# Stick-breaking attention summed by parts in a one-core encoder step

## The chip, the cores and the metric

The kernel runs on one core of a Trainium2 chip. The metric is the device time of one execution in microseconds (us); a kernel is run several times and the median is taken. A profiled execution gives the trace. The engines are named as in the profile: PE is the matrix engine, PEld its weight loads, DVE the vector engine, ACT the scalar engine, POOL the third elementwise engine, SP the engine that issues the DMAs.

## The reference, cut to what matters

One layer: a projection of 1056 rows (1024 prompt, 32 sample) by 1024 features, of which eight heads of 64 go to attention, then convolution, gates, an output projection, a feed-forward part and an embedding gate. The change touches the attention over the 1024 prompt rows:

```python
z = jnp.einsum('bqhd,bkhd->bhqk', q, k) * scale
mask = k_pos[None, :] < q_pos[:, None]
log_1m = jnp.where(mask, jax.nn.log_sigmoid(-z), 0.0)
tail = lax.cumsum(log_1m, axis=3, reverse=True) - log_1m
a = jnp.where(mask, jnp.exp(jax.nn.log_sigmoid(z) + tail), 0.0)
out = jnp.einsum('bhqk,bkhd->bqhd', a, v)
```

So the weight of key s is sigmoid(z_s) times the product of sigmoid(-z_j) over the later keys j that the query may see. All of it is float32. The keys and values of the prompt and the samples are outputs too.

## The kernel before

Nearly every matrix product is made of three: each float32 operand is split into a rounded part and a remainder ("hi" and "lo"), and hi·hi, hi·lo and lo·hi are summed in PSUM. The program has stages: the input projection (`seven`, by a scheme with seven half-size products for each pair of output blocks, some 264 columns a matmul), then attention, then the projections `oc` and `oa` of the two branches, `wo`, and the feed-forward part and the rest.

**Order.** Under `manual_schedule` the instructions of ACT, PE, DVE and POOL run in the order in which Python writes them. SP's order is chosen by the framework's scheduler. In the projection stage `run(body)` takes one step of the matrix work (for `seven`, 12 matmuls) and then one step of every generator in the list `side`, so a `yield` in `values` or `keys_or_queries` means: 12 matmuls later. The values are the sets i7 (blocks p = 0 and 1) and i10 (blocks 2 and 3). Their generator `values(p, m)` runs while the next set is multiplied; block 1 starts six steps after block 0.

**Values before.** `m` holds 128 value features (two heads) by 1056 rows. `values` scales it, waits three steps, transposes eight 128×128 blocks on PE through PSUM (`pt_v`) into `vt`, writes `vt` to the output, and for each of the two heads splits `vt` into a tile `vs` (hi in columns 0 to 63, lo in 64 to 127), which goes to the DRAM scratch `vd`. Attention reads it back as `vv`. The 32 sample rows are transposed too (`pts_v`).

**Buffers.** Tiles made by `blk` share a pool of 34 buffers of one size (`bpool`). A tile that takes over a buffer waits for everything that still reads it, a DMA out of it included. The transposes' PSUM tiles (`tps`) have two buffers.

**Attention before.** There are 64 steps (p, j, i): block p, head j, and 128 queries i against L = 128(i+1) keys. In step n, in the order "LSAFBFG", `scores` (S) makes z for step n and two sigmoids of it, r = sigmoid(-z) and s = sigmoid(z), and POOL sets the last 128 columns of both where a key is not earlier than the query; `weigh` (L) scans r of step n-1 from its last key backwards into running products and multiplies s by the products one to the right; `flip` (A and B) transposes s of step n-2 on PE and splits it into hi and lo parts `at`; for odd i, `gather` (G) multiplies the `at` of 256 queries by `vv`, lo and hi of each key block, into `av`, whose halves are added (through `avl`) into `oT`. For the lower 128 of the 256 queries the last key block is all masked: POOL sets that half to zero and the matmul still takes 256 columns. At F the generator `work` puts gate matmuls (`ps_g`, later `ps_pw`) between; how many go into which step is set by `pace`, with a load for each step made from four constants. The 32 sample queries (`samples`: `zs`, `ss`, `sr`, `avs`) are done beside the first steps.

Of the kernel before, what the change touches and what calls it, by code (L numbers as in the profile page):

```python
# [49 lines left out]
def tile_step(  # L50
# [1 line left out]
    tc: tile.TileContext,  # L52
    xf, xr_, pT, ckT, cache_v, vecs,
    w_in, w_attn_out, w_conv_out, w_o, w_up, w_down, w_ple_gate, w_ple,
    y_main, y_last, k_out, v_out, v_sample, conv_out,
):


# [8 lines left out]
    def blk(name, dt=F32, shape=None):  # L67
        return bpool.tile(shape or [P, T], dt, tag="B", name=name)
# [364 lines left out]
    ch, cl = [], []  # L433
    st, cst = {}, {}
    qsT, ksT, vsT = ([cpool.tile(sh, F32, name=f"{nm}s{p}") for p in range(4)] for nm, sh in (("q", [P, DEC]), ("k", [P, DEC]), ("v", [DEC, P])))

    def run_units(units):

# [63 lines left out]
    def values(p, m):  # L502
        scaled(m)
        for _ in range(3):
            yield
        tm = blk(f"vt{p}", F32, [P, 8, P])
        for q0 in (0, 4):
            pt = tps.tile([P, 4, P], F32, tag="tp", name=f"pt_v{p}_{q0}")
            for i in range(4):
                nc.tensor.transpose(pt[:, i, :], m[:, (q0 + i) * P : (q0 + i + 1) * P], ident)  # L510
            nc.scalar.copy(tm[:, q0 : q0 + 4, :], pt)
            yield
        pt = tps.tile([P, 4, P], F32, tag="tp", name=f"pts_v{p}")
        nc.tensor.transpose(pt[:DEC, 0, :], m[:, SEQ:], ident)
        nc.scalar.copy(vsT[p], pt[:DEC, 0, :])
        nc.sync.dma_start(v_out[p], tm)
        nc.sync.dma_start(v_sample[p], vsT[p])
        for j in range(2):
            vs = blk(f"vs{p}{j}", F32R, [P, 8, P])
            src = tm[:, :, 64 * j : 64 * j + 64]  # L520
            nc.scalar.copy(vs[:, :, 0:64], src)
            dve(vs[:, :, 64:128], src, vs[:, :, 0:64].bitcast(F32), op=sub)
            nc.sync.dma_start(vd[p, j], vs.bitcast(F32).rearrange("p a c -> p (a c)"))
            yield

    def conv_in(nb, m):

# [227 lines left out]
    def scores(p, j, i):  # L755
        q, kk = live["q", p, j, i // 2], st["k", p, j]
        L = P * (i + 1)
        nh = 1 if L <= 512 else 2
        W = L // nh
        z = zps.tile([P, 2, 512], F32, tag="z", name=f"z{p}{j}{i}")  # L760
        tq = slice((i % 2) * P, (i % 2) * P + P)
        for h in range(nh):
            zz = z[:, h, :W]
            ks = kk[:, h * W : (h + 1) * W]
            nc.tensor.matmul(zz, q[:, 0, tq], ks, start=True, stop=False)
            nc.tensor.matmul(zz, q[:, 1, tq], ks, start=False, stop=True)
        zv = z[:, :nh, :W]
        s = blk(f"s{p}{j}{i}", F32, [P, SEQ])
        r = apool.tile([P, SEQ], F32, tag="R", name=f"r{p}{j}{i}", bufs=3)
        for o, sign in ((r, -1.0), (s, 1.0)):  # L770
            nc.scalar.activation(o[:, :L].rearrange("p (h w) -> p h w", h=nh), zv, AF.Sigmoid, scale=sign)  # L771
        earlier(r[:, L - P : L], 1.0)
        earlier(s[:, L - P : L], 0.0)
        live[p, j, i] = (s, r, L)

    def earlier(a, fill):

# [2 lines left out]
            a, a, pattern=[[-1, n]], compare_op=ALU.is_gt, fill=fill, base=0, channel_multiplier=1  # L780
        )

    def sticks(s, r, L):


        rev = r[:, L - 1 :: -1] if L == r.shape[-1] else r[:, :L][:, ::-1]
        nc.vector.tensor_tensor_scan(rev, rev, rev, 1.0, ALU.mult, ALU.bypass)  # L787
        nc.vector.tensor_tensor(s[:, : L - 1], s[:, : L - 1], r[:, 1:L], op=ALU.mult)

    def weigh(p, j, i):  # L790
        sticks(*live[p, j, i])

    def turned(shape, name):

# [2 lines left out]

    def flip(p, j, i):
        nm = f"{p}{j}{i}"
        s, _, L = live.pop((p, j, i))  # L800
        c, u = i // 2, i % 2
        if u == 0:
            live["A"] = [[None, None], [None, None]]
            for s_ in range(2):
                nblk = min(4, 2 * c + 2 - 4 * s_)
                if nblk <= 0:
                    continue
                for hl in range(2):
                    if nblk == 4:
                        a = blk(f"at{nm}{hl}{s_}", F32R, [P, 4, 256])  # L810
                    else:
                        a = apool.tile([P, 2, 256], F32R, tag="A2", name=f"at{nm}{hl}{s_}", bufs=2)
                    live["A"][hl][s_] = a
        A = live["A"]
        for b0 in range(0, i + 1, 4):
            nb = min(4, i + 1 - b0)
            pt = turned([P, 4, P], f"pa{nm}{b0}")
            for b in range(nb):
                nc.tensor.transpose(pt[:, b, :], s[:, (b0 + b) * P : (b0 + b + 1) * P], ident)
# [3 lines left out]
            nc.vector.tensor_tensor(al, pt[:, :nb, :], ah.bitcast(F32), op=ALU.subtract)  # L823
            if b0 == 0 and i >= 4:
                yield
        if u == 0:
            b = i + 1
            for hl in range(2):
                nc.gpsimd.memset(A[hl][b // 4][:, b % 4, 0:P].bitcast(F32), 0.0)
        else:  # L830
            live["A", p, j, c] = A

    def gather(p, j, c):
        A = live.pop(("A", p, j, c))
        vv = st["v", p, j]
        av = turned([P, 256], f"av{p}{j}{c}")
        n = 2 * c + 2
        for b in range(n):
            for hl in range(2):
                nc.tensor.matmul(  # L840
                    av, vv[:, b, :], A[hl][b // 4][:, b % 4, :],
                    start=(b == 0 and hl == 0), stop=(b == n - 1 and hl == 1),
                )
# [5 lines left out]
        nc.scalar.copy(lo, av[64:128, :])  # L849
        nc.vector.tensor_tensor(  # L850
            oT[p][64 * j : 64 * j + 64, c * 256 : (c + 1) * 256], av[0:64, :], lo, op=ALU.add
        )


# [108 lines left out]


    osT = tpool.tile([P, 4, DEC], F32, tag="os", name="osT", bufs=1)

    def samples():
        cv = blk("cv", F32, [P, 2, SB])
# [49 lines left out]
    def pace():  # L1018
# [6 lines left out]
        load, own = [], []  # L1025
        for n in range(ns + 2):
            a, b, c = size(n - 1), size(n - 2), size(n - 3)
            v = 0.4 * a + 0.15 * b + 0.3 + 0.4 * (c % 2 == 0 and c > 0)
            load.append(max(v, 1.6) + 3.0 * (n == 6) + 0.5 * (n == 4))
            own.append(0.24 * size(n) + 0.11 * b + 0.24 * c * (c % 2 == 0))  # L1030
        for more in (0, 1, 2, 3, None):
# [799 lines left out]
```

## Time and profile before

| | us |
|---|---|
| median of three runs | 1565.12 |
| lowest, highest run | 1562.71, 1565.26 |
| span of the profiled execution | 1565.4 |
| PE busy in it | 1533.8 |
| DVE busy | 1101.6 |
| ACT busy | 769.2 |
| POOL busy | 393.5 |

The span is that of the profiled execution, from its first to its last instruction; the runs are whole executions without the profile. Attention lies between about 331 and 600 us of the span. Busy times of PE are longer than what its matmuls cost, since a matmul's record covers its way through the array while the next one has already started: the distance from start to start is the cost. Waits of PE show best at its weight loads (PEld).

### The profile page before, as it was taken

What the parts mean: (1) busy time and instruction counts of PE and PEld (TensorE: products, weight loads), DVE (VectorE), ACT (ScalarE), POOL (GpSimd) and SP (SyncE); (2) the same over time, 40 slices, a digit from 0 to 9 for tenths busy, and PEclk for the clock granted to TensorE, in tenths of its full rate; (3) what the DMA queues carried; (4) which work ended last, traced back from release to release, by engine and by line L of the source; (5) the groups of instructions that cost most, each with busy time, mean ns of one, the idle gap of its engine ahead of it and who ended that gap; (6) DMA issues with size and microseconds to landing.
All of it is one profiled execution on the core that took longest, in us unless ns stands there. A gap on an engine that the chain in (4) does not pass through costs nothing.

```text
span 1565.4 us, 29674 instructions
## 1 busy us (share of the span) xinstructions
PE 1533.8 (98%) x11842; PEld 1519.2 (97%) x11842; DVE 1101.6 (70%) x1437; ACT 769.2 (49%) x1361; POOL 393.5 (25%) x412
## 2 busy tenths in 40 slices
PE   7999999999999999999999999999999999999996
PEld 7999999999999999999999999999999999999996
DVE  7568565666888888675667555555577986789866
ACT  6644444444666675323255555555643334444544
POOL 1223332022334334101312222222020221013353
PEclk9999999999999999999999999999999999999998
DMA  6512455373334366334544433444786897583433
GB/s 222 205 52 107 170 195 199 85 242 106 105 115 142 118 210 242 117 109 171 187 173 151 149 138 141 144 152 152 263 309 200 275 336 256 187 271 104 140 118 118
DMA packets 109803, 268.98 MB, mean 172 GB/s; under 512 B 12992, under 2 KB 28992, under 8 KB 109664
## 3 DMA queue, kind: packets, MB, share of 16 engines
q1 hardware_dynamic: 109520, 267.05, 50.4%
q8 instruction: 93, 1.52, 0.4%
q14 instruction: 46, 0.38, 0.1%
q10 hardware_dynamic: 144, 0.03, 0.0%
HBM read 186.31 MB, written 80.72 MB: 171 GB/s over the span
## 4 chain that ended last, share of the span: by engine, by line
PE 53%; DVE 3%; issue 1%; POOL 1%; ACT 1%; DMA 1%; SPq 0%; DVEq 0%; POOLq 0%; ACTq 0%
PE ps_dn L1432 7%; PE ps_dn L1430 7%; PE ps_dn L1431 7%; PE ps_A11u L204 4%; PE ps_A11u L203 4%; PE ps_A11u L205 4%; PE ps_wo L107 2%; PE ps_wo L108 2%; PE ps_wo L109 2%; PE ps_S1u L204 2%; PE ps_S1u L203 2%; PE ps_S1u L205 2%; DMA s<-gd 1%; PE ps_oa L109 1%; PE ps_oa L107 1%
## 5 line engine op out<-in xcount | busy, mean ns | idle before, releaser
L1431 PE MATMUL ps_dn<-fl,whi_dn 128*128 128x264 f32 x896 | 254.7, 284 | 0.2 <-DVE fl L1339 0.2
L1432 PE MATMUL ps_dn<-fh,wlo_dn 128*128 128x264 f32 x896 | 254.8, 284 | 0.0
L1430 PE MATMUL ps_dn<-fh,whi_dn 128*128 128x264 f32 x896 | 254.7, 284 | 0.0
L1431 PEld LDWEIGHTS ps_dn<-fl,whi_dn 128*128 128x128 f32 x896 | 168.5, 188 | 0.4 <-DVE fl L1339 0.4
L1432 PEld LDWEIGHTS ps_dn<-fh,wlo_dn 128*128 128x128 f32 x896 | 168.7, 188 | 0.0
L1430 PEld LDWEIGHTS ps_dn<-fh,whi_dn 128*128 128x128 f32 x896 | 168.6, 188 | 0.0
L645 PE MATMUL ps_g<-B,whi_g 128*128 128x264 f32 x384 | 115.9, 302 | 0.0
L646 PE MATMUL ps_g<-B,whi_g 128*128 128x264 f32 x384 | 109.9, 286 | 0.0
L647 PE MATMUL ps_g<-B,wlo_g 128*128 128x264 f32 x384 | 109.7, 286 | 0.0
L779 POOL TENSOR_SCALAR_AFFINE_SELECT r<-r 128x128 f32<-128x128 f32 x64 | 45.8, 715 | 206.8 <-ACT r L771 204.9
L190 POOL TENSOR_TENSOR s_u<-raw_u,raw_u 128x512 f32<-128x512 f32 x30 | 44.0, 1468 | 187.5 <-DVE slS_u L153 185.8
L1323 DVE TENSOR_TENSOR wlo_dn<-raw_dn,whi_dn 128x1024 fp32r<-128x1024 f32 x40 | 71.0, 1776 | 25.5 <-ACT whi_dn L1317 24.9
L1372 POOL TENSOR_TENSOR c<-c,rs 128x528 f32<-128x528 f32 x16 | 26.7, 1668 | 244.3 <-DVE c L1439 122.6
L1317 ACT CAST whi_dn<-raw_dn 128x1024 fp32r<-128x1024 f32 x40 | 42.0, 1051 | 93.5 <-PE ps_dn L1431 75.3
L787 DVE TENSOR_TENSOR_SCAN r<-r 128x128 f32<-128x128 f32 (+3 forms) x64 | 86.9, 1357 | 1.1 <-POOL r L779 0.6
L190 POOL TENSOR_TENSOR s_i<-raw_i,raw_i 128x512 f32<-128x512 f32 x24 | 33.0, 1376 | 189.5 <-DVE slS_i L153 156.2
L645 PEld LDWEIGHTS ps_g<-B,whi_g 128*128 128x128 f32 x384 | 73.0, 190 | 0.0
L646 PEld LDWEIGHTS ps_g<-B,whi_g 128*128 128x128 f32 x384 | 73.0, 190 | 0.0
L647 PEld LDWEIGHTS ps_g<-B,wlo_g 128*128 128x128 f32 x384 | 72.8, 190 | 0.0
L1339 DVE TENSOR_TENSOR fl<-mr,fh 128x1056 fp32r<-128x1056 f32 x56 | 69.8, 1247 | 4.3 <-ACT fh L1334 4.3
L204 PE MATMUL ps_A11u<-T,shS_u 128*128 128x264 f32 x240 | 68.6, 286 | 0.0
L203 PE MATMUL ps_A11u<-T,shS_u 128*128 128x264 f32 x240 | 68.6, 286 | 0.0
(430 smaller groups left out, 5548.5 us busy)
## 6 DMA issues: line engine op xcount, KB each, us to landing
raw_dn<-in_w_down_dram SPq DMA_DIRECT2D x56, 512.0 KB, 4.5
mr<-mdT SPq DMA_DIRECT2D x32, 528.0 KB, 5.5
raw_u<-in_w_up_dram SPq DMA_DIRECT2D x32, 512.0 KB, 3.5
raw_i<-in_w_in_dram SPq DMA_DIRECT2D x28, 512.0 KB, 4.6
mdB<-m SPq DMA_DIRECT2D x48, 264.0 KB, 2.4
mr<-mdB SPq DMA_DIRECT2D x24, 528.0 KB, 6.5
raw_pg<-in_w_ple_gate_dram SPq DMA_DIRECT2D x17, 512.0 KB, 3.5
gd<-sg SPq DMA_DIRECT2D x16, 528.0 KB, 2.8
```

Source lines behind the costliest of these rows:

```text
L190: f()
L203: nc.tensor.matmul(p_, wh[:, k, :], o[:, 0, c], start=new and n == 0, stop=False, **on)
L204: nc.tensor.matmul(p_, wh[:, k, :], o[:, 1, c], start=False, stop=False, **on)
L205: nc.tensor.matmul(p_, wl[:, k, :], o[:, 0, c], start=False, stop=z, **on)
L645: nc.tensor.matmul(ps, wh[:, k, :], o[:, 0, q], start=i == 0 and k == 0, stop=False)
L646: nc.tensor.matmul(ps, wh[:, k, :], o[:, 1, q], start=False, stop=False)
L647: nc.tensor.matmul(ps, wl[:, k, :], o[:, 0, q], start=False, stop=i == 3 and k == 3)
L787: nc.vector.tensor_tensor_scan(rev, rev, rev, 1.0, ALU.mult, ALU.bypass)
L1323: dve(lo, raw, hi.bitcast(F32), op=sub)
L1430: nc.tensor.matmul(ps, hi[:, j, :], oh, start=j == 0, stop=False)
L1431: nc.tensor.matmul(ps, hi[:, j, :], ol, start=False, stop=False)
L1432: nc.tensor.matmul(ps, lo[:, j, :], oh, start=False, stop=j == NP_ - 1)
```

## The change

With P_s the product of sigmoid(-z_j) over the keys from s on, the weight of key s is P_(s+1) − P_s. The sum over the keys of weight times value is therefore the last value of the block plus the sum of P_s times (v_(s-1) − v_s), with −v_0 for the first key. The scan makes P_s; masked keys have the factor one.

In `values`, a tile `dv` takes the differences of neighbouring rows of `m` (one DVE subtraction over 1023 columns and one ACT copy for the first column), and `dv` is transposed in place of `m`. The transposed blocks are split straight out of PSUM into both heads' `vs`, 256 columns at a time. The last value of each 128-row block goes through a small tile `ve` and DRAM to `vend`, which attention reads. The value output is written from `m` untransposed, and the host turns it; the separate output of the sample values is gone. In attention the second sigmoid, its masking, the multiplication behind the scan and the zeroing are gone, the transposes read r, `gather` takes 128 columns for the last key block, and `avl` is made by two ACT instructions that add `vend`. Four r buffers replace three, and s takes none of the pool. `pace` has other constants. The samples keep the old form.

```diff
@@ values
-        tm = blk(f"vt{p}", F32, [P, 8, P])
+        nc.sync.dma_start(v_out[p], m)
+        d = blk(f"dv{p}", F32, [P, SEQ])
+        dve(d[:, 1:], m[:, : SEQ - 1], m[:, 1:SEQ], op=sub)
+        nc.scalar.activation(d[:, 0:1], m[:, 0:1], AF.Copy, scale=-1.0)
+        ve = wpool[0].tile([64, 2, 8], F32, tag="ve", name=f"ve{p}", bufs=1)
+        for j in range(2):
+            nc.scalar.copy(ve[:, j, :], m[64 * j : 64 * j + 64, P - 1 : SEQ : P])
+        nc.sync.dma_start(ved[:, p], ve.rearrange("p a c -> p (a c)"))
+        pt = tps.tile([P, 4, P], F32, tag="tp", name=f"pts_v{p}")
+        nc.tensor.transpose(pt[:DEC, 0, :], m[:, SEQ:], ident)
+        nc.scalar.copy(vsT[p], pt[:DEC, 0, :])
+        yield
+        vs = [blk(f"vs{p}{j}", F32R, [P, 8, P]) for j in range(2)]
         for q0 in (0, 4):
             pt = tps.tile([P, 4, P], F32, tag="tp", name=f"pt_v{p}_{q0}")
             for i in range(4):
-                nc.tensor.transpose(pt[:, i, :], m[:, (q0 + i) * P : (q0 + i + 1) * P], ident)
-            nc.scalar.copy(tm[:, q0 : q0 + 4, :], pt)
-            yield
...
-        nc.sync.dma_start(v_out[p], tm)
-        nc.sync.dma_start(v_sample[p], vsT[p])
+                nc.tensor.transpose(pt[:, i, :], d[:, (q0 + i) * P : (q0 + i + 1) * P], ident)
+            for j in range(2):
+                src, to = pt[:, :, 64 * j : 64 * j + 64], vs[j][:, q0 : q0 + 4, :]
+                nc.scalar.copy(to[:, :, 0:64], src)
+                dve(to[:, :, 64:128], src, to[:, :, 0:64].bitcast(F32), op=sub)
+            yield
         for j in range(2):
-            vs = blk(f"vs{p}{j}", F32R, [P, 8, P])
-            src = tm[:, :, 64 * j : 64 * j + 64]
-            nc.scalar.copy(vs[:, :, 0:64], src)
-            dve(vs[:, :, 64:128], src, vs[:, :, 0:64].bitcast(F32), op=sub)
-            nc.sync.dma_start(vd[p, j], vs.bitcast(F32).rearrange("p a c -> p (a c)"))
-            yield
+            nc.sync.dma_start(vd[p, j], vs[j].bitcast(F32).rearrange("p a c -> p (a c)"))
@@ scores, weigh
-        s = blk(f"s{p}{j}{i}", F32, [P, SEQ])
-        r = apool.tile([P, SEQ], F32, tag="R", name=f"r{p}{j}{i}", bufs=3)
-        for o, sign in ((r, -1.0), (s, 1.0)):
-            nc.scalar.activation(o[:, :L].rearrange("p (h w) -> p h w", h=nh), zv, AF.Sigmoid, scale=sign)
+        r = apool.tile([P, SEQ], F32, tag="R", name=f"r{p}{j}{i}", bufs=4)
+        nc.scalar.activation(r[:, :L].rearrange("p (h w) -> p h w", h=nh), zv, AF.Sigmoid, scale=-1.0)
         earlier(r[:, L - P : L], 1.0)
-        earlier(s[:, L - P : L], 0.0)
-        live[p, j, i] = (s, r, L)
+        live[p, j, i] = (r, L)
...
     def weigh(p, j, i):
-        sticks(*live[p, j, i])
+        left_over(*live[p, j, i])
@@ flip, gather
-        if u == 0:
-            b = i + 1
-            for hl in range(2):
-                nc.gpsimd.memset(A[hl][b // 4][:, b % 4, 0:P].bitcast(F32), 0.0)
-        else:
+        if u:
             live["A", p, j, c] = A
...
-        for b in range(n):
-            for hl in range(2):
-                nc.tensor.matmul(
-                    av, vv[:, b, :], A[hl][b // 4][:, b % 4, :],
-                    start=(b == 0 and hl == 0), stop=(b == n - 1 and hl == 1),
-                )
+        turns = [(b, hl) for b in range(n - 2) for hl in range(2)]
+        turns += [(n - 2, 0), (n - 1, 0), (n - 1, 1), (n - 2, 1)]
+        for k, (b, hl) in enumerate(turns):
+            q0 = P * (b == n - 1)
+            nc.tensor.matmul(
+                av[:, q0:], vv[:, b, :], A[hl][b // 4][:, b % 4, q0:],
+                start=k == 0, stop=k + 1 == len(turns),
+            )
...
-        nc.scalar.copy(lo, av[64:128, :])
+        for u in range(2):
+            q = slice(u * P, u * P + P)
+            nc.scalar.activation(lo[:, q], av[0:64, q], AF.Identity, bias=vend[:, p, 8 * j + 2 * c + u : 8 * j + 2 * c + u + 1])
         nc.vector.tensor_tensor(
-            oT[p][64 * j : 64 * j + 64, c * 256 : (c + 1) * 256], av[0:64, :], lo, op=ALU.add
+            oT[p][64 * j : 64 * j + 64, c * 256 : (c + 1) * 256], av[64:128, :], lo, op=ALU.add
         )
...
+    vend = tpool.tile([64, 4, 16], F32, tag="ve", name="vend", bufs=1)
+    nc.sync.dma_start(vend, ved)
@@ pace
-            v = 0.4 * a + 0.15 * b + 0.3 + 0.4 * (c % 2 == 0 and c > 0)
+            v = 0.29 * a + 0.17 * b + 0.35 + 0.42 * (c % 2 == 0 and c > 0)
```

How this stands on the engines, at the three places that the prediction speaks of. In the rows, a number at the end of a name is the buffer's, L is the line of the respective program, and the shape is that of the output.

**DVE around the differences of block 1.** The names: `m2_i7` is block 1's `m`, `m1_i8` and `m2_i8` the outputs of the next set, `ps_A11i8` and `ps_S1i8` its PSUM groups, `sl..` and `wlo` remainders of its weights. Before:

```order
187 L479 TENSOR_TENSOR m2_i7_2043<-m2_i7_2043,rs_120 128x1056
188 L239 TENSOR_TENSOR m1_i8_2289<-ps_A12i8_1_2444,p1_i81_2292 128x264
189 L244 TENSOR_TENSOR m2_i8_2290<-ps_A11i8_0_2297,s5_i80_2295 128x264
190 L153 TENSOR_TENSOR slS1_i9_2473<-raw_i9_1_2165,shS1_i9_2471 128x512
191 L244 TENSOR_TENSOR m2_i8_2290<-ps_A11i8_1_2320,s5_i81_2296 128x264
192 L249 TENSOR_TENSOR m1_i8_2289<-u2_i80_2293,ps_S1i8_0_2335 128x264
```

With the change:

```order
190 L480 TENSOR_TENSOR m2_i7_2044<-m2_i7_2044,rs_120 128x1056
191 L239 TENSOR_TENSOR m1_i8_2290<-ps_A12i8_1_2452,p1_i81_2293 128x264
192 L244 TENSOR_TENSOR m2_i8_2291<-ps_A11i8_0_2298,s5_i80_2296 128x264
193 L153 TENSOR_TENSOR slS1_i9_2481<-raw_i9_1_2166,shS1_i9_2479 128x512
194 L244 TENSOR_TENSOR m2_i8_2291<-ps_A11i8_1_2321,s5_i81_2297 128x264
195 L509 TENSOR_TENSOR dv1_2497<-m2_i7_2044 128x1023
196 L249 TENSOR_TENSOR m1_i8_2290<-u2_i80_2294,ps_S1i8_0_2336 128x264
197 L527 TENSOR_TENSOR vs10_2520<-pt_v1_0_2522,vs10_2520 128x4x64
```

The subtraction into `dv1` now stands between two evacuations of PSUM. Its buffer is the one that `vs00` (block 0, head 0) had, so it waits until `vs00`'s DMA to `vd` has landed; `vt1` before, an ACT copy, took over the same buffer and had the same wait. The same holds for `dv3` and `vs20`.

**SP at the same place.** `raw_i10_1` and `raw_i11_0` are weights of later sets, half a megabyte each. Before:

```order
65 L516 DMA out_v_out_dram<-vt0_2364 128x1024
66 L517 DMA out_v_sample_dram<-vs0_157 32x128
67 L89 DMA raw_i10_1_2423<-in_w_in_dram 128x1024
68 L523 DMA vd_146<-vs00_2417 128x1024
69 L523 DMA vd_146<-vs01_2439 128x1024
70 L89 DMA raw_i11_0_2697<-in_w_in_dram 128x1024
```

With the change:

```order
65 L507 DMA out_v_out_dram<-m1_i7_2043 128x1056
66 L514 DMA ved_161<-ve0_2369 64x16
67 L89 DMA raw_i10_1_2433<-in_w_in_dram 128x1024
68 L89 DMA raw_i11_0_2712<-in_w_in_dram 128x1024
69 L530 DMA vd_146<-vs00_2394 128x1024
70 L530 DMA vd_146<-vs01_2395 128x1024
```

The transfer of `vs00` now stands behind one more weight transfer.

**DVE in two steps of attention.** `r106` is the r of block 1, head 0, i = 6. Before:

```order
393 L850 TENSOR_TENSOR oT1_5275<-av101_5376,avl101_5385 64x256
394 L787 SCALAR_TENSOR_TENSOR r106_5333<-r106_5333 128x896
395 L788 TENSOR_TENSOR s106_5332<-s106_5332,r106_5333 128x895
396 L823 TENSOR_TENSOR at10410_5341<-pa1050_5403,at10400_5340 128x4x128
397 L823 TENSOR_TENSOR at10411_5343<-pa1054_5423,at10401_5342 128x2x128
398 L787 SCALAR_TENSOR_TENSOR r107_5396<-r107_5396 128x1024
399 L788 TENSOR_TENSOR s107_5395<-s107_5395,r107_5396 128x1023
```

With the change:

```order
383 L856 TENSOR_TENSOR oT1_5217<-av101_5310,avl101_5319 64x256
384 L789 SCALAR_TENSOR_TENSOR r106_5270<-r106_5270 128x896
385 L829 TENSOR_TENSOR at10410_5276<-pa1050_5334,at10400_5275 128x4x128
386 L829 TENSOR_TENSOR at10411_5278<-pa1054_5353,at10401_5277 128x2x128
387 L789 SCALAR_TENSOR_TENSOR r107_5329<-r107_5329 128x1024
```

One DVE instruction less stands between a step's scan and the transposes of that step, and between one scan and the next. PE's own list keeps all its instructions; gate matmuls move between neighbouring steps in groups of six, and six more of them now stand ahead of the samples' first matmuls.

More of the change, by code (lines that the diff above doesn't have):

```diff
@@ L54, in tile_step @@
     w_in, w_attn_out, w_conv_out, w_o, w_up, w_down, w_ple_gate, w_ple,
-    y_main, y_last, k_out, v_out, v_sample, conv_out,
+    y_main, y_last, k_out, v_out, conv_out,
 ):
@@ L435, in tile_step @@
     qsT, ksT, vsT = ([cpool.tile(sh, F32, name=f"{nm}s{p}") for p in range(4)] for nm, sh in (("q", [P, DEC]), ("k", [P, DEC]), ("v", [DEC, P])))
+    ved = dpool.tile([64, 4, 16], F32, name="ved")
     def run_units(units):
@@ L781, in earlier, with left_over, sticks @@
         )
-    def sticks(s, r, L):
+    def left_over(r, L):
         rev = r[:, L - 1 :: -1] if L == r.shape[-1] else r[:, :L][:, ::-1]
         nc.vector.tensor_tensor_scan(rev, rev, rev, 1.0, ALU.mult, ALU.bypass)
+    def sticks(s, r, L):
+        left_over(r, L)
         nc.vector.tensor_tensor(s[:, : L - 1], s[:, : L - 1], r[:, 1:L], op=ALU.mult)
     def weigh(p, j, i):
-        sticks(*live[p, j, i])
+        left_over(*live[p, j, i])
     def turned(shape, name):
@@ L799, in flip @@
         nm = f"{p}{j}{i}"
-        s, _, L = live.pop((p, j, i))
+        s, L = live.pop((p, j, i))
         c, u = i // 2, i % 2
@@ L1800 @@
         "k_out": (4, P, T),
-        "v_out": (4, P, 8, P),
-        "v_sample": (4, DEC, P),
+        "v_out": (4, P, T),
         "conv_out": (4, 2, P, 2),
@@ L1821 @@
     k = o["k_out"].reshape(SB, T).T
-    v = o["v_out"].transpose(2, 1, 0, 3).reshape(SEQ, SB)
-    vs = o["v_sample"].transpose(1, 0, 2).reshape(DEC, SB)
+    v = o["v_out"].reshape(SB, T).T
     c = o["conv_out"].transpose(1, 3, 0, 2).reshape(2, 2, CW)
@@ L1826 @@
         (y[:SEQ], (1, SEQ, D)), (y[SEQ:], (1, DEC, D)),
-        (k[:SEQ], (1, 1, SEQ, NH, HD)), (v, (1, 1, SEQ, NH, HD)), (c[0], (1, 1, 2, CW)),
-        (k[SEQ:], (1, 1, DEC, NH, HD)), (vs, (1, 1, DEC, NH, HD)), (c[1], (1, 1, 2, CW)),
+        (k[:SEQ], (1, 1, SEQ, NH, HD)), (v[:SEQ], (1, 1, SEQ, NH, HD)), (c[0], (1, 1, 2, CW)),
+        (k[SEQ:], (1, 1, DEC, NH, HD)), (v[SEQ:], (1, 1, DEC, NH, HD)), (c[1], (1, 1, 2, CW)),
     )
```

3 lines of the change are left out of this document (removed).

## The prediction

> **What bounds the kernel now.** I read the page first: how busy each engine is.
>
> ```profile
> PE 1533.8 (98%) x11842; PEld 1519.2 (97%) x11842; DVE 1101.6 (70%) x1437; ACT 769.2 (49%) x1361; POOL 393.5 (25%) x412
> ```
>
> PE and its weight loads fill the span; DVE has a third of it free. A share over the whole span doesn't say whether attention itself is limited by something else, so the next view is busy time by stage: the projections, attention, the two branch projections, the feed-forward part. The columns are the window, its length, PE, PEld, DVE, ACT, POOL, the granted clock, the DMA share and GB/s.
>
> ```profile
> 0.00:331.00 331.00, 320.14 (x2598) 318.22 (x2598) 217.36 (x294) 158.78 (x324) 75.04 (x54) 1.00 0.46 157
> 331.00:600.00 269.00, 265.88 (x2043) 256.84 (x2044) 220.33 (x286) 170.60 (x355) 92.19 (x208) 0.99 0.47 150
> 600.00:650.00 50.00, 47.06 (x291) 46.48 (x290) 38.44 (x42) 21.95 (x25) 21.90 (x8) 1.00 0.56 198
> 650.00:1440.00 790.00, 789.59 (x6200) 788.53 (x6199) 535.02 (x674) 357.44 (x560) 151.30 (x96) 1.00 0.56 192
> ```
>
> In attention DVE is busy for 220 of 269 us, far more than its share elsewhere, but PE is still busier. So PE's own waits there are the ceiling of what lighter DVE, ACT and POOL work can give back. The view of waits for that window, at the weight loads, gives all of them (total, times, longest):
>
> ```profile
> PEld pa L819 <- DVE s L788: 2.3, 6, 0.7
> PEld zs L981 <- DVE kk L977: 1.2, 1, 1.2
> PEld z L765 <- issue: 1.2, 2, 0.7
> PEld ps_pw L727 <- DVE pw0l L711: 0.7, 1, 0.7
> PEld ps_pw L725 <- ACT em L728: 0.5, 1, 0.5
> PEld av L840 <- DVE at L823: 0.5, 1, 0.5
> PEld zs L981 <- issue: 0.4, 2, 0.2
> PEld pa L819 <- issue: 0.2, 1, 0.2
> ```
>
> That is 7.0 us of 269, and 3.1 us is 0.2% of the kernel, which is about what its runs can tell from no change. A big gain is not on offer.
>
> **Work taken off engines that aren't the bound.** The rows of what goes, and of the ACT copy that is replaced (count, then min/median/max ns):
>
> ```profile
> L788 DVE TENSOR_TENSOR s<-s,r x64: 292/822/1306, 334.4 to 588.0; 128x127 f32<-128x127 f32 x8, 128x255 f32<-128x255 f32 x8, 128x383 f32<-128x383 f32 x8, 128x511 f32<-128x511 f32 x8
> L771 ACT ACTIVATE s<-z x64: 260/646/1024, 332.2 to 582.4; 128x128 f32<-128x128 f32 x8, 128x256 f32<-128x256 f32 x8, 128x384 f32<-128x384 f32 x8, 128x512 f32<-128x512 f32 x8
> L779 POOL TENSOR_SCALAR_AFFINE_SELECT s<-s x64: 287/294/2355, 332.7 to 583.5; 128x128 f32<-128x128 f32 x64
> L829 POOL MEMSET at<- x64: 200/203/208, 337.2 to 583.9; 128x128 f32 x64
> L849 ACT COPY avl<-av x32: 369/370/373, 346.3 to 598.6; 64x256 f32<-64x256 f32 x32
> ```
>
> DVE loses 64 × 0.82 = 53 us, ACT 64 × 0.65 = 41 us, POOL at least 64 × (0.29 + 0.20) = 32 us. ACT gets 32 more instructions for `avl`, each over 128 of the 256 columns; even at the whole copy's 0.37 us that is 12 us. All of it lies under PE's 266 us; without PE's work on top it would be worth those tens of us, but as it is only the waits above can go.
>
> *Waits for the multiplication (2.3 us).* One of the six, PE's rows and DVE's:
>
> ```profile
> 400.39 0.27 PE L766 MATMUL z<-ks,q 128*128 128x128 f32 x1
> 401.01 0.66 PE L819 MATMUL pa<-ident,s 128*128 128x128 f32 x4 [0.34 <-DVE s L788]
> 399.78 1.17 DVE L788 TENSOR_TENSOR s<-s,r 128x895 f32<-128x895 f32 x1
> ```
>
> PE stands ready at 400.5; the multiplication ends at 400.95. The transposes of r need only the scan before it, done by 399.8. Each such wait is at most 0.7, and the instruction that goes is 0.82 in the median, so I take all 2.3. What is late next there is the ACT and DVE split of the transposes, which a gate group covers.
>
> *Waits of the embedding units (0.7 + 0.5).* `pw0l` stands on DVE behind a long multiplication, and the `em` copy on ACT behind a second sigmoid of up to 1.02. Each obstacle is longer than the wait: −1.2. The wait of `av` for `at` (0.5) has neither ahead of it: kept.
>
> *The samples (1.2).* They wait for `kk`, whose last part comes by DMA. The DMA's place doesn't move, while PE's list has six gate matmuls more ahead of the samples than before. Six starts at 0.12 us (worked out below for 256 columns) are 0.7: −0.7, with 0 as the other end, if the DMA is later too. The first `z` waits for an evacuation that stays: nothing.
>
> **Half blocks.** In 32 gathers two matmuls each go from 256 to 128 columns. The rows for both widths:
>
> ```profile
> 331.26 0.19 PEld L765 LDWEIGHTS z<-ks,q 128*128 128x128 f32 x1 [0.70 <-issue]
> 331.37 0.19 PEld L766 LDWEIGHTS z<-ks,q 128*128 128x128 f32 x1
> 331.48 0.19 PEld L645 LDWEIGHTS ps_g<-B,whi_g 128*128 128x128 f32 x1
> 331.59 0.19 PEld L646 LDWEIGHTS ps_g<-B,whi_g 128*128 128x128 f32 x1
> 483.34 1.11 PE L840 MATMUL av<-at,vv 128*128 128x256 f32 x8
> ```
>
> The two at 331.26 have 128 columns in the same number format, and their loads start 0.11 apart, as the loads of the 264-wide ones behind them do. Eight 256-wide ones take 1.11, the last 0.28 of it its own, so (1.11 − 0.28)/7 = 0.119 each. The gain is 64 × (0.119 − 0.11) = −0.6, not half of each matmul: the weight load is still whole.
>
> **The values, where something is added.** Block 1's differences wait for a DMA (and block 3's), and PE's transposes wait for the differences.
>
> ```profile
> 196.39 1.23 DVE L99 TENSOR_TENSOR wlo_i<-raw_i,whi_i 128x1024 fp32r<-128x1024 f32 x1 [0.74 <-ACT whi_i L98]
> 198.24 1.26 SPq L523 DMA_DIRECT2D vd<-vs  x2
> 199.59 0.64 SPq L89 DMA_DIRECT2D raw_i<-in_w_in_dram  x1
> DMA to landing us min/median/max: 2.6/4.2/4.8
> 201.86 0.43 DVE L244 TENSOR_TENSOR m_i<-ps_A11i,s_i 128x264 f32<-128x264 f32 x1 [0.25 <-PE ps_A11i L205]
> 202.77 0.59 ACT L511 COPY vt<-pt_v 128x512 f32<-128x512 f32 x1 [4.44 <-DMA vd<-vs]
> 203.56 0.60 PE L510 MATMUL pt_v<-ident,m_i 128*128 128x128 f32 x4
> L498 DVE TENSOR_TENSOR m_i<-m_i,qh x4: 1210/1214/1220, 153.8 to 218.4; 128x1024 fp32r<-128x1024 f32 x4
> L562 DVE TENSOR_TENSOR m_i<-m_i,cvh x4: 1250/1305/2268, 136.8 to 332.5; 128x1056 fp32r<-128x1056 f32 x4
> ```
>
> Today ACT waits 4.4 us for that landing and PE doesn't notice: only a copy is behind it. With the change PE's first transposes of the differences come where the second four stand now, less the four that turned into one: 203.56 − 0.35 = 203.2. `vs00` is ready when DVE has done `wlo` (till 197.6) and one short subtraction, about 198.1; SP first issues the weight (0.64, released by the same `wlo`), so `vd` goes out at about 198.4. It lands 4.2 later, 202.6, after DVE has finished with L244 (202.3). The subtraction, at L498's 1.21, ends at 203.8, and PE has waited 0.6. Behind the waiting subtraction stands L249, an evacuation of PSUM whose group PE needs again only in the next set. Two blocks: +1.2. The ends: landing in 2.6 leaves L244 as the last, 0.3 each, +0.6; landing in 4.8 and a subtraction at 2.27, which DVE shows at times, 2.3 each, +4.6. I take the middle by the medians. Blocks 0 and 2 have no such DMA ahead.
>
> The rest of `values` on ACT and DVE (splits out of PSUM, two short copies) has room in the stage's 217 of 331 us of DVE. `vend` is one small DMA read ahead of the first queries; it could delay them by its issue, but the first `z` waits for an evacuation instead, so I set it at nothing.
>
> **Sum.** −2.3 − 1.2 − 0.7 − 0.6 + 1.2 = −3.6. Against the profiled execution's 1565.4 that is 1561.8. That execution lies 0.3 over the median of the runs, 1565.12; by the same step the median becomes **1561.5**. Beyond 650 us nothing is touched and PE has no gap to lose.
>
> **Rivals.**
>
> *A matmul's cost goes by its width.* Then a half block saves half of 0.119, 64 × 0.06 = 3.8 in place of 0.6: 1558.3. The rows at 331.26 speak against it. The Trainium skill, TensorE: Matmul & The Clock Gate, "Back-to-back issue gap", has an isolated gap of columns / 2.4 + 2.5 ns, an estimate of 53 ns saved for each, 3.4 in all, and says beside it that in a stream the weight loads count too. By the first half of that sentence the time would be some 1558.7; the rows here side with the second.
>
> *Waits that move.* PE's list is as full as before. If the chain from scores over sigmoid, mask, scan, transposes and split ends up waiting at the split, or the six gate matmuls are missed elsewhere, half of the 4.2 us of waits comes back: −1.5, 1563.6, no change that can be told. For it: each removed wait was under 0.7, so small shifts make new ones. Against: DVE has 53 us less to do.
>
> *The values' DMA holds PE.* The place is `dv1` and `dv3`. Each us that `vd` lands later is a us of PE, twice, since transposes, and all matmuls behind them, stand in order. From 0.6 + 1.8 late each, PE loses the whole 4.8 gain; from 4 us each the kernel is measurably slower. If the weight ahead of it must land first and `vd` needs another 4.2 after that, the weight issued at 197.7 lands at 201.9, `vd` at 206.1, the subtraction ends at 207.3, 4.1 late each: +8.2 − 4.8 = +3.4, 1568.5. Against: at 198.24 and 199.59 transfers overlapped and landed within 4.8.
>
> *The clock.* One stretch of attention runs throttled:
>
> ```profile
> 360.00:400.00 40.00, 40.00 (x309) 38.37 (x309) 28.34 (x37) 22.72 (x49) 11.92 (x26) 0.91 0.28 87
> ```
>
> 0.09 × 40 is 3.6 us of clock, beside the samples' small matmuls, which stay. Where it falls may move the time either way by up to that; it widens the range.
>
> **How the numbers follow.** The sum, 0.52, of which 0.40 beyond 3.1 us; width, 0.10; moved waits, 0.25; the values' DMA, 0.13. So faster by over 0.2%: 0.40 + 0.10 = 0.50; within 0.2%: 0.12 + 0.25 = 0.37; slower: 0.13. The sum's own range, from +0.6 to +4.6 at the values and 0 at the samples, is 1560.9 to 1565.6, less up to 2 us of clock below; for 8 in 10 I take 1557.5, past the width rival, to 1566.5.
>
> **What would show it.** PE's waits for 331 to 600 us: no L788, no `pw0l`, no `em`, `zs` at half; total near 3. New PE waits for `dv` at about 203 and 266, 0.6 each. The 128-column `av` matmuls 0.11 apart. DVE busy in attention near 170. Wrong would be: waits of PE for `r` or `at` of over 2 us, `dv` waits over 2 us each, or a changed gap after 600 us.

## The result, and the profile after

| | runs | median us | lowest, highest |
|---|---|---|---|
| before | 15 | 1564.97 | 1562.71, 1569.58 |
| changed | 15 | 1565.87 | 1562.44, 1570.11 |

The ratio is 1.0007, with a 95% interval of 0.9997 to 1.0016: no change that can be told. The forecast was 3.6 us less.

One thing about the profiled executions first. The changed kernel's has a span of 1563.0 and is the run of 1564.82: a run is its span and some 1.8 us (e12: 1563.0 and 1564.74). So the profile of before, with 1565.4, belongs by estimate to an execution of about 1567.2, which lies 2 us over its median, and not 0.3 as the prediction had it. The spans differ by −2.4 and the medians by +0.9; what the change did has to be read place by place and from runs, not from the two spans.

The page's busy line of the changed kernel:

```profile
PE 1533.8 (98%) x11842; PEld 1520.8 (97%) x11842; DVE 1057.3 (68%) x1385; ACT 741.3 (47%) x1341; POOL 352.8 (23%) x284
```

Busy time by stage, with the same columns as in the prediction: the first values, attention, the branch projections.

```profile
200.00:220.00 20.00, 18.13 (x138) 17.93 (x137) 12.77 (x18) 8.50 (x23) 6.05 (x4) 0.91 0.46 184
...
331.00:600.00 269.00, 267.70 (x2081) 259.73 (x2080) 173.66 (x222) 147.12 (x326) 51.93 (x80) 0.99 0.49 154
...
600.00:650.00 50.00, 50.00 (x313) 50.00 (x312) 38.16 (x45) 22.23 (x25) 21.72 (x8) 1.00 0.58 208
```

The first and the last of these windows in the profile of before:

```profile
200.00:220.00 20.00, 20.00 (x167) 19.98 (x167) 14.99 (x18) 11.08 (x23) 6.38 (x4) 1.00 0.60 243
...
600.00:650.00 50.00, 47.06 (x291) 46.48 (x290) 38.44 (x42) 21.95 (x25) 21.90 (x8) 1.00 0.56 198
```

In attention DVE went from 220 to 174 us, and PE is busier. Two windows changed that lie outside attention. At 200 to 220 PE lost 1.9 us of busy time and the mean granted clock is 0.91 instead of 1.00, and at 600 to 650 PE has no gap any more.

What the weight loads wait for in attention, 331 to 600 us (total, times, longest):

```profile
PEld z L771 <- issue: 1.2, 2, 0.7
PEld av L844 <- DVE at L829: 0.6, 1, 0.6
PEld zs L989 <- DVE kk L985: 0.6, 1, 0.6
PEld zs L989 <- issue: 0.5, 2, 0.3
PEld zs L989 <- DVE r L789: 0.5, 1, 0.5
PEld ps_pw L733 <- DVE pw0l L717: 0.4, 1, 0.4
PEld pa L825 <- DVE r L789: 0.3, 1, 0.3
```

That is 4.1 us, where 7.0 stood before. The waits for the multiplication are gone but for 0.3 on the scan. In the branch projections the changed kernel has none, and before had two that the prediction didn't list:

```profile
PEld ps_oa L109 <- DVE wlo_oa L99: 2.0, 1, 2.0
PEld ps_oc L109 <- DVE wlo_oc L99: 1.5, 1, 1.5
```

So by its waits the changed kernel gained 2.9 + 3.5 us behind 331 us. It gave most of that back ahead of 331 us. There its new entry among the waits of the weight loads is this:

```profile
PEld pt_v L523 <- ACT vs L517: 3.9, 2, 2.0
```

The first of the two pauses, in the timeline (start, length, what ran, and in brackets the idle time ahead and what ended it), DVE's rows, then ACT's, SP's and PE's:

```profile
202.00 0.43 DVE L244 TENSOR_TENSOR m_i<-ps_A11i,s_i 128x264 f32<-128x264 f32 x1
203.65 1.22 DVE L509 TENSOR_TENSOR dv<-m_i 128x1023 f32<-128x1023 f32 x1 [1.22 <-DMA vd<-vs]
...
203.66 0.20 ACT L510 ACTIVATE dv<-m_i 128x1 f32<-128x1 f32 x1 [4.30 <-DMA vd<-vs]
...
204.07 0.25 ACT L517 COPY vs<-pts_v 32x128 f32<-32x128 f32 x1
...
198.59 1.07 SPq L530 DMA_DIRECT2D vd<-vs  x2
...
202.87 0.28 PE L205 MATMUL ps_S1i<-B,slS_i 128*128 128x264 f32 x1
205.02 0.82 PE L523 MATMUL pt_v<-ident,dv 128*128 128x128 f32 x4 [1.87 <-DVE dv L509]
```

The list of waits names ACT's copy (L517), but that was done at 204.32. PE's own row has it right: the transposes follow the subtraction, which ends at 204.87, and the subtraction follows the landing of `vd`. SP issued it at 198.59, DVE was free at 202.4, and it landed at 203.65. All matmuls behind the transposes stood still from 203.0 to 205.0; the second pause, at 270, is 1.8 long. The trace's records of the granted clock show 0.5 from 205.31 on, for 3.41 us, which costs up to 1.7 more (half of it). The profile of before has no such window there. But its window beside the samples' matmuls (379.18 on) is 6.83 us long, where that of the changed kernel (386.22 on) is 3.41. So these two executions lost the same to the clock, and the spans differ by about what the waits say: −6.4 + 3.9 = −2.5, measured −2.4. That the changed kernel loses more to the clock has to be read from all its runs (the table of clocks below).

### The profile page after: what moved, and what is told of

Same layout as the page of the kernel before. It is cut to its first block, busy times and chain, and to the rows that moved or that the text cites. A ratio compares the mean times of both kernels' runs of the same rounds, so it can differ in the third digit from the quotient of the medians.

```text
span 1563.0 us, 29320 instructions
## 1 busy us (share of the span) xinstructions
PE 1533.8 (98%) x11842; PEld 1520.8 (97%) x11842; DVE 1057.3 (68%) x1385; ACT 741.3 (47%) x1341; POOL 352.8 (23%) x284
## 4 chain that ended last, share of the span: by engine, by line
PE 88%; DVE 4%; ACT 2%; DMA 2%; issue 2%; POOL 1%; SPq 0%; DVEq 0%; POOLq 0%; ACTq 0%
PE ps_dn L1440 7%; PE ps_dn L1439 7%; PE ps_dn L1438 7%; PE ps_A11u L204 4%; PE ps_A11u L203 4%; PE ps_A11u L205 4%; PE ps_g L652 3%; PE ps_g L651 3%; PE ps_g L653 3%; PE ps_A11i L205 3%; PE ps_A11i L203 3%; PE ps_A11i L204 3%; PE av L844 2%; PE ps_wo L108 2%; PE ps_wo L107 2%; PE ps_wo L109 2%
```

## The experiments

The theory: attention and what follows gained some 5 us, and the two pauses with the clock behind them took it back. The rivals: attention gained nothing by itself, and the medians only show the clock's chance. All runs are compared with runs of the kernel before on the same chip; its median was 1564.5 to 1565.0 in the three groups of runs (e1 to e4, e5 to e8, e9 to e12).

| run | edit | median us | ratio to before, 95% |
|---|---|---|---|
| e1 | transposes of the differences one step later | 1560.50 | 0.9969 (0.9959–0.9978) |
| e2 | differences of a pair in one buffer | 1569.46 | 1.0037 (1.0023–1.0051) |
| e3 | attention part alone | 1560.19 | 0.9969 (0.9957–0.9981) |
| e4 | values part alone | 1571.52 | 1.0049 (1.0035–1.0063) |
| e5 | e1 with whole last blocks | 1561.43 | 0.9976 (0.9968–0.9984) |
| e6 | e1 with r in the large buffers | 1559.12 | 0.9959 (0.9946–0.9972) |
| e7 | e1 with DVE's multiplication as idle work | 1561.18 | 0.9977 (0.9968–0.9987) |
| e8 | e1 with the samples' matmuls spread | 1559.89 | 0.9962 (0.9949–0.9976) |
| e9 | e1 with the old pace | 1561.81 | 0.9979 (0.9970–0.9988) |
| e10 | before with the new pace | 1567.36 | 1.0017 (1.0008–1.0025) |
| e11 | e6 and e8 together | 1557.62 | 0.9961 (0.9947–0.9976) |
| e12 | before with the samples' matmuls spread | 1564.72 | 1.0001 (0.9991–1.0012) |

**e1: give the subtraction a step of cover.**

```diff
         nc.scalar.copy(vsT[p], pt[:DEC, 0, :])
         yield
+        yield
         vs = [blk(f"vs{p}{j}", F32R, [P, 8, P]) for j in range(2)]
```

> The changed kernel, with the transposes of the differences one place (24 matmuls of TensorE) later behind the subtraction. Theory (the two pauses of TensorE of 2.0 and 1.8 us at the differences of blocks 1 and 3, and a half-clock window that can follow such a pause, give back what attention gained): no gap over 0.3 us at 203 and 270 us, 3.9 us less, up to 1.7 more where the window behind the first pause goes too; median 1560.5 to 1562. Rival (the attention part itself gains almost nothing, and what is lost at the values would be waited for elsewhere): the gaps go, the median stays at 1565 to 1566.

DVE's and PE's rows at the same place:

```profile
204.42 1.23 DVE L509 TENSOR_TENSOR dv<-m_i 128x1023 f32<-128x1023 f32 x1 [0.67 <-DMA vd<-vs]
...
205.91 0.28 PE L205 MATMUL ps_S1i<-B,slS_i 128*128 128x264 f32 x1
206.03 0.60 PE L524 MATMUL pt_v<-ident,dv 128*128 128x128 f32 x4
```

DVE still waits for the DMA; PE doesn't, and no half-clock window stands at 205. The median is 1560.5, 0.31% under before, where the changed kernel is 0.07% over: a difference of 0.38%, 5.9 us, of which the pauses are 3.9. With one `yield` the change gains 4.9 us by the ratio, more than the 3.6 that were forecast for all of it.

**e2: take the DMA out of the subtraction's way.**

```diff
-        d = blk(f"dv{p}", F32, [P, SEQ])
+        if p % 2 == 0:
+            dvs[p // 2] = blk(f"dv{p}", F32, [P, SEQ])
+        d = dvs.pop(p // 2) if p % 2 else dvs[p // 2]
```

> The changed kernel, with the differences of blocks 1 and 3 written into the buffer of the differences of blocks 0 and 2, so that they wait for no DMA. Theory (the landing of vd is what is late): the subtraction follows DVE's evacuations at 202.4, the pauses shrink to 0.6 or 0.8 each, 2.4 us less, 1563.4, and less still if the half-clock window needs the long pause. Rival (DVE's queue is what is late): the pauses stay at 1.8 to 2.0 and the time at 1565 to 1566.

Both expectations were wrong. The pauses grew to 3.4 and 3.3 us:

```profile
204.35 0.43 DVE L244 TENSOR_TENSOR m_i<-ps_A11i,s_i 128x264 f32<-128x264 f32 x1 [2.52 <-DMA vd<-vs]
204.70 0.68 DVE L153 TENSOR_TENSOR slS_i<-raw_i,shS_i 128x512 fp32r<-128x512 f32 x1
205.30 0.43 DVE L244 TENSOR_TENSOR m_i<-ps_A11i,s_i 128x264 f32<-128x264 f32 x1
205.64 1.22 DVE L513 TENSOR_TENSOR dv<-m_i 128x1023 f32<-128x1023 f32 x1
...
203.52 0.28 PE L205 MATMUL ps_S1i<-B,slS_i 128*128 128x264 f32 x1
207.00 0.63 PE L527 MATMUL pt_v<-ident,dv 128*128 128x128 f32 x4 [3.20 <-DVE dv L513]
```

The buffer out of which the DMA reads now went to the output tile of the next set, so its evacuation (L244) waits for the landing, and stands ahead of the subtraction on DVE with two more instructions between. The landing is what is late, as the theory said. But DVE's queue carries the wait wherever the buffer goes, and one entry earlier in it costs more. The time is 1569.5.

**e3 and e4: each half alone.** In e3 `values` turns and splits `m` as before the change (the last values still go to `vend`), with the changed attention; in e4 the changed `values` feeds the attention of before. The core of e3's edit (e4 has the changed `values` whole, and `scores`, `weigh`, `flip`, `gather` and `pace` of before):

```diff
-        d = blk(f"dv{p}", F32, [P, SEQ])
-        dve(d[:, 1:], m[:, : SEQ - 1], m[:, 1:SEQ], op=sub)
...
+        tm = blk(f"vt{p}", F32, [P, 8, P])
...
-                nc.tensor.transpose(pt[:, i, :], d[:, (q0 + i) * P : (q0 + i + 1) * P], ident)
+                nc.tensor.transpose(pt[:, i, :], m[:, (q0 + i) * P : (q0 + i + 1) * P], ident)
+            nc.scalar.copy(tm[:, q0 : q0 + 4, :], pt)
```

> The attention part of the change alone: the values are turned and split as before the change, no differences are taken (so the sum by parts is over values instead of differences). Theory: attention and what follows it are worth some 4 to 5 us, 1560 to 1562, as in the run with the later transposes; TensorE's waits at 620 and 645 us are gone here too. Rival (attention gains almost nothing): 1564 to 1566.

> The values part of the change alone: attention as before the change, over values that are differences. Theory: the two pauses of TensorE at 203 and 270 appear, 3.9 us, with up to 1.7 of clock behind them: 1569 to 1570.5. Rival (the pauses are hidden later or are a matter of the attention part): 1564 to 1566.

e3 is 0.9969, the same as e1: apart from the two pauses the values part costs nothing that shows. Of its expectation one line failed: a wait of 1.4 at `wlo_oc` is left, that at `wlo_oa` is gone. e4 is 0.49% slower, 7.7 us, and its pauses are longer, in the same entry of its waits:

```profile
PEld pt_v L524 <- ACT vs L518: 4.7, 2, 2.4
```

Its 1571.5 lies over what was expected, by 1 us, and its 7.7 over what the pauses explain, by 3. The rest shows in the clock. The mean granted clock over all runs of a kernel:

| kernel | pauses at the values | runs | mean granted clock |
|---|---|---|---|
| before, in the three groups of runs | none | 19, 23, 27 | 0.9942, 0.9944, 0.9943 |
| e1, e3 | none | 10, 9 | 0.9945, 0.9940 |
| changed | 2.0, 1.8 | 15 | 0.9933 |
| e4 | 2.4, 2.3 | 6 | 0.9925 |
| e2 | 3.4, 3.3 | 6 | 0.9915 |

The longer the pauses, the lower the clock. From e1 to the changed kernel it is 0.0012, an estimated 1.9 us of 1563; with the 3.9 of the pauses that makes 5.8 of the 5.9 measured. From before to e4 it is 0.0017, 2.6 us, and with 4.7 that makes 7.3 of 7.7. A straight line through the changed kernel's own fifteen runs gives 1.1 us for each 0.001 of clock, 1.3 for 0.0012. The clock scatters from run to run (0.990 to 0.996 in the changed kernel), so each of these shares has a standard error of some 0.8 us: the pauses are shown, the clock's share behind them is an estimate.

**e5: what the half blocks are worth.**

```diff
-        turns = [(b, hl) for b in range(n - 2) for hl in range(2)]
-        turns += [(n - 2, 0), (n - 1, 0), (n - 1, 1), (n - 2, 1)]
+        turns = [(b, hl) for b in range(n) for hl in range(2)]
...
-            q0 = P * (b == n - 1)
+            q0 = 0
```

(and the zeroing in `flip` again.)

> The run with the later transposes, with the last block of each gather again 256 columns wide (its first half set to zero on GpSimd as before the change). Theory (a 128-column matmul stands 0.0856 us ahead of its successor in the mean, a 256-column one 0.119): 64 x 0.033 = 2.1 us more than with half blocks, 1562 to 1563. Rival (as predicted, 0.11 each): 0.6 more, 1561. Rival (cost goes by width): 3.8 more, 1564.

The group of these matmuls in the changed kernel (median of a record's length, then how many of each width):

```profile
L844 PE MATMUL av<-at,vv x320: 218/281/384, 352.1 to 597.4; 128*128 128x256 f32 x128, 128*128 128x128 f32 x32
```

From start to start in the same trace, the first of the two 128-column matmuls stands 0.060 ahead of the next (median of 32), the second 0.112, and a 256-column one 0.119. By these the half blocks save 64 × (0.119 − 0.086) = 2.1 us. By the ratios the run is 0.07%, 1.1 us, slower than e1, with intervals that overlap: it fits 0.6 and 2.1, and speaks against 3.8.

**e6 and e7: what ended the waits at 620 and 645 us?** e6 takes r from the large buffers, as s was:

```diff
-        r = apool.tile([P, SEQ], F32, tag="R", name=f"r{p}{j}{i}", bufs=4)
+        r = blk(f"r{p}{j}{i}", F32, [P, SEQ])
```

e7 keeps three r buffers of their own and puts this behind the scan:

```diff
+        x = apool.tile([P, SEQ], F32, tag="X", name=f"x{p}{j}{i}", bufs=1)
+        nc.vector.tensor_tensor(x[:, : L - 1], r[:, : L - 1], r[:, 1:L], op=ALU.mult)
```

> The run with the later transposes, with r of attention taken from the 34 large buffers, as s was before the change, and no buffers of its own. Theory (the waits at 620 and 645 us went because s no longer takes these buffers, so that the gates' read-backs are issued sooner): TensorE's wait at wlo_oa of 2 us and perhaps the one at wlo_oc are back, the read-backs around 607 us are issued some us later, 2 to 3.5 us more, 1562.5 to 1564. Rival (they went because DVE has less to do): no such wait, 1560.5.

> The run with the later transposes, with DVE's second multiplication put back as work that nobody reads (the product of r and its shifted self into a buffer of its own, 64 instructions, 53 us of DVE). Theory (53 us of DVE were under TensorE's work, and only the waits for the multiplication itself counted): DVE is busy for some 225 us of attention again, TensorE's waits there grow by under 1 us, 1560 to 1561.5. Rival (DVE's load sets the waits, through the splits that stand behind it in its queue and the weights of the branch projections): the waits of before are back, 2 to 4 us more, 1563 to 1565.

In e6 SP issues the gates' read-backs at 601.0, as in e1 (600.9); no wait at `wlo_oa` came back, only 0.7 at `wlo_oc`, and the time didn't rise. The idea that the freed buffers did it falls. e7's attention window and its longest wait there:

```profile
331.00:600.00 269.00, 266.63 (x2057) 258.18 (x2056) 221.62 (x287) 145.39 (x324) 49.28 (x81) 0.99 0.48 152
...
PEld ps_pw L734 <- DVE pw0l L718: 1.5, 1, 1.5
```

DVE is loaded as before (222 us, before 220), and the wait for `pw0l` grew from 0.4 to 1.5. Otherwise PE hardly notices 46 us more of DVE work, and the branch projections have no wait. DVE's load isn't what ended those either. By the ratios the time is 1.3 us over e1, less than these runs can tell apart.

**e9 and e10: the pace.** What is left is the four constants, exchanged both ways:

```diff
-            v = 0.29 * a + 0.17 * b + 0.35 + 0.42 * (c % 2 == 0 and c > 0)
+            v = 0.4 * a + 0.15 * b + 0.3 + 0.4 * (c % 2 == 0 and c > 0)
```

> The run with the later transposes, with the constants of the pace as before the change (0.4, 0.15, 0.3, 0.4). Nine matmuls of the branch projections stand ahead of the last gather then, with the new constants three. Theory (where the fill work stands against the last gather sets how late DVE's splits and the next weights come): TensorE's waits at wlo_oc and wlo_oa are back, 1.5 to 3.5 us, 1562 to 1564. Rival (they hang on the engines' lighter work): no such waits, 1560 to 1561.

> The kernel before, with the constants of the pace as in the change and nothing else. Four matmuls of the branch projections stand ahead of the last gather, in place of eleven. Theory: the waits at wlo_oc and wlo_oa of 3.5 us go, those for the multiplication stay or grow by up to 1, 1561.5 to 1563. Rival (lighter work): both stay, 1564 to 1566.

e9's two longest waits of weight loads from 331 to 660 us, those for the branch projections and the samples:

```profile
PEld ps_oc L109 <- DVE wlo_oc L99: 1.6, 1, 1.6
PEld zs L990 <- DVE r L790: 1.4, 1, 1.4
```

And e10's, the kernel before with the new pace:

```profile
PEld pa L819 <- DVE s L788: 5.0, 12, 0.9
PEld z L765 <- ACT s L771: 2.4, 3, 1.6
...
PEld ps_oc L109 <- DVE wlo_oc L99: 0.5, 1, 0.5
```

The new pace takes 3.0 of the 3.5 us away in the old kernel. The old pace in the new kernel shows 1.6 at `wlo_oc`, but that says little, since kernels with the new pace have anything there from nothing (e1, e7) to this (e2):

```profile
PEld ps_oc L109 <- DVE wlo_oc L99: 1.9, 2, 1.4
```

The wait at `wlo_oa` is clearer. It is 1.9 to 2.2 us in the three profiles that have both the old attention and the old pace (before, e4, e12) and absent from all others. So either part alone ends it: the new pace, which changes how much fill work stands ahead of the last gathers (e10), or the lighter attention (e9). By which of its parts the lighter attention does so stays open. The pace is not free, though: in the old kernel the new pace more than doubles the waits for the multiplication, 2.3 to 5.0, and adds 2.4 for the second sigmoid: e10 is 0.17% slower. The expectation of e10 missed that. With the lighter attention the new pace brings no such waits: 0.3 for the scan in the changed kernel, and none for a sigmoid.

**e8, e11, e12: the block of small matmuls.** Each of the samples' eight heads becomes a piece of its own:

```diff
+                if (j, p) != (1, 3):
+                    yield
...
             for op in ORDER:
+                if n in (11, 12) and op in "LFG":
+                    next(sample, None)
```

> The run with the later transposes, with the samples' 24 small matmuls issued in eight pieces among the gate and attention matmuls of two steps instead of in one block. Theory (a stretch of 4.6 us of small matmuls lets the clock fall, as a pause of 2 us does): no half-clock window between 376 and 400 us in the profile, 1.7 to 3.4 us less, 1557 to 1559. Rival (the window does not hang on where they stand): a window of 3.41 us or more stays there, 1560.5.

> Later transposes, the samples' small matmuls spread, and r from the large buffers, together. Theory (the three are independent, and r's place is worth nothing): as with the spread alone, 1558.5 to 1560. Rival (r's place is worth 1 us by itself, as the run with it alone could suggest): 1557.5 to 1558.5.

> The kernel before, with nothing but the samples' 24 small matmuls spread in eight pieces. Theory (half-clock window behind the block of small matmuls, 6.83 us long in the profile of before, is worth 1.7 to 3.4 us wherever it falls): no window between 376 and 400 us, 1561.5 to 1563.5. Rival (the window moves elsewhere, or the pieces cost what it gives): 1564 to 1566.

The window of 380 to 400 us in e1:

```profile
380.00:400.00 20.00, 20.00 (x148) 19.09 (x148) 12.61 (x15) 9.99 (x21) 3.63 (x5) 0.91 0.26 87
```

and in e8:

```profile
380.00:400.00 20.00, 20.00 (x160) 19.03 (x160) 13.24 (x15) 10.48 (x22) 4.63 (x5) 1.00 0.29 94
```

The half-clock window at the block is gone in e8, e11 and e12, and the mean clock over the runs rose by 0.0013 in e8 (0.9945 in e1 to 0.9958) and by 0.0012 in e12 (0.9943 to 0.9955), an estimated 2 us each. Whether the time followed can't be told for e8: by the ratios it is 1.1 us under e1, and its interval is 2 us either way. e12 is not faster than before (1.0001, at best 0.9991, 1.4 us). So the theory holds for the clock and isn't shown for the time; what takes the 2 us back in e12 was not found, and it is a reason to take the clock's share in the loss above as an estimate only. e11 has the lowest median of all, 1557.6, in the range of its rival, but its interval, like those of e6 and e8, holds e1's ratio, so that r's place is not shown to be worth anything. What can be said is that the change with the transposes a step later beats the kernel before by 0.31% and the changed one by 0.38%.

## Why the prediction was right and wrong

Its range held the time, near the upper end; its forecast of a gain wasn't borne out. A change within 0.2% did stand there at 0.37, but 0.25 of that was for waits that move. What took the gain back was the values' DMA, to which the forecast had given the slower outcomes.

**The attention terms: right in sum, not one by one.** −4.8 was forecast without the values; e3 measured 0.31%, −4.9 (3.0 to 6.7). That they agree so closely is luck: three of the terms were too large, one perhaps too small, and one was missing. Taken singly, in the profiles:
- The multiplication: 2.3 became 0.3, −2.0 of −2.3.
- The embedding units: `em` went; at `pw0l` 0.4 stayed, −0.8 of −1.2. That DVE's multiplication was the obstacle fits e7, where work of its size stands there again and the wait is 1.5.
- The samples: the wait for `kk` halved as forecast, but 0.5 for the scan's r and 0.5 of issue stand beside it. 1.6 before, 1.6 after: nothing, where −0.7 was taken. This was the moved-waits rival, in this one place.
- Half blocks: the row chosen, 0.11 between two loads, holds for the second of a pair only. The first costs 0.060. Over the 32 pairs the loads there start 0.108 to 0.120 apart throughout (medians). The first 128-column matmul starts 0.116 after its load, the second only 0.057 after its own. So the first lets the matmuls catch up with the loads, once. The term lies between −0.6 and −2.1, e5 can't tell more closely. The Trainium skill, TensorE: Matmul & The Clock Gate, "Back-to-back issue gap", gives some 81 ns for a 128-column matmul in a stream with its loads; the mean here, 86 ns, agrees with that; by that figure the term would have been an estimated −2.4.
- Missing from the sum: the waits at `wlo_oc` and `wlo_oa`, 3.5 us. The view of waits that the sum used ended at 600 us, and "Beyond 650 us nothing is touched" passed over the 50 between, though the prediction's own row for 600 to 650 us has PE busy for only 47.06 of 50. There the new constants of the pace (e10) and the lighter attention (e9) act.

**The values: the step that failed.** "PE has waited 0.6. […] Two blocks: +1.2" was 2.0 and 1.8, and with the clock an estimated 5.8 in all. The mechanism, place and instruction were right; the size of the term was wrong. At the first pause the difference is made up of four things. The landing came 5.06 us after the issue and 4.2 was taken, the median of before; the eight landings of `vd` went from 2.6/4.2/4.8 (min, median, max) to this, for a reason that wasn't tried:

```profile
DMA to landing us min/median/max: 2.7/4.8/5.5
```

The issue was at 198.59 instead of 198.4. PE came to the transposes at 203.0 instead of 203.2, and from the end of the subtraction to the first transpose 0.15 passes, which was left out. Together 0.86 + 0.19 + 0.2 + 0.15 = 1.4 on top of the 0.6. All four were small against the quantities they belong to, but the term was a difference of two nearly equal times, so they all went into it.

**The rival that came true.** "From 0.6 + 1.8 late each, PE loses the whole 4.8 gain", the text says of the values' DMA, at a chance of 0.13. The pauses were 1.3 longer each than taken, and the lower clock accounts, by estimate, for the rest. The clock was a rival only as chance ("may move the time either way"); in e1 to e4 the mean clock falls with the length of the pauses.

**What it said would show it.** Held: no L788, no `em`, DVE near 170 in attention (174). Not: `zs` at half, no `pw0l`, a total near 3 (4.1), the 128-column matmuls 0.11 apart. Of the signs that would make it wrong, one came, a changed gap after 600 us; the `dv` waits of 2.0 and 1.8 stopped just short of another, "over 2 us each".

## What to carry to other kernels

A new tile in a rotating pool inherits the transfer that still reads its buffer. When such a tile feeds the matrix engine, put the matrix work a step later than the engine in between needs, and look who gets the buffer instead before moving it. Price a pause of PE with the clock behind it, by estimate half as much again here, and when a term is the difference of two nearly equal times, take its whole range as its price.

## What the runs showed of the hardware

A pause of PE of 2 us can be followed by a halved clock. In the 14 profiles taken, a pause of 1.8 to 2.4 us at 142 us, which all of them have, is followed within 4 us by a window of 3.41 us at half clock in seven (e1, e2, e3, e5, e6, e7, e9), and not in the others. The same happened after the pause at 203 in the changed kernel, at 270 in e2 and at 648 in e4, while those at 270 in the changed kernel, at 203 in e2 (3.4 us long) and at 203 and 270 in e4 had none behind them, nor had the pause of 1.8 to 2.0 us at about 1480 us that all 14 have. A stretch of 4.6 us of the samples' 32-column matmuls without a pause (380.98 to 385.58 in the changed kernel, the window from 386.22) did it too: a window starts inside it or within 1 us of its end in all 11 profiles where they stood in one block, and in none of the 3 where they were spread. No other half-clock window stands between 14 and 1540 us in any of the profiles. The Trainium skill, TensorE: Matmul & The Clock Gate, "The HAM clock gate", has the window as 3413 ns and free-running, which agrees with 3.41 and 6.83 and with its being a matter of chance. The Trainium skill's rule on the same page, "HAM oscillation", is no idle gaps over some 3.4 us; by these runs gaps of 2 us are already too long to be safe.

Of two neighbouring 128-column matmuls behind 256-column ones the first stands 0.060 us ahead of the next and the second 0.112, while their weight loads keep a distance of 0.108 to 0.120 throughout.
